# Two load buffers of their own for modulation weights, and a down projection that moves 512 columns

## The chip, the cores and the metric

The kernel runs on one core of a Trainium2 chip, as one program. The metric is device time in microseconds, from the start to the end of an execution. Of the core's engines, TensorE (PE) multiplies, VectorE (DVE) and ScalarE (ACT) work element by element, GpSimd (POOL) does little here, and SyncE (SP) only issues transfers: all of the kernel's transfers stand in its one queue, in program order, and one that waits for a buffer holds those behind it.

## What is computed

Two layers of a backbone over 512 latent tokens and 256 context tokens with 1024 channels. Each layer has shift, scale and gate vectors from a small product with `w_mod` ("modulation"), three token mixers (retention, attention, mLSTM) with a gated merge and an output projection, and a gated MLP:

```
mod_l = split((silu_c @ w_mod[l] + b_mod[l])[:, None, :], 6)
pl = split_proj(modulate(x, mod_l[0], mod_l[1]) @ w_in[l] + b_in[l])
...
x = layer_norm(alpha * x + mod_l[2] * mix_l, ln1_g[l], ln1_b[l])
ffn_l = conv_ffn(modulate(x, mod_l[3], mod_l[4]), w_up[l], conv_w[l], conv_b[l], w_down[l])
x = layer_norm(alpha * x + mod_l[5] * ffn_l, ln2_g[l], ln2_b[l])
```

In `conv_ffn` the hidden layer has 2816 features, and its last product is `(silu(g) * a) @ w_down`. In layer 0 context tokens are carried along (768 tokens); layer 1 needs outputs for the 512 latent tokens alone.

## The kernel before

**Products.** Every large product is made in three passes of a reduced 32-bit format: the operand is split into a high part and a rest (`xh`, `xl`; `ah`, `al`; weights `wh`, `wl`), and high x high, high x rest, rest x high are summed in PSUM. A block of weights, up to 128 x 1024 numbers or 512 KB, comes by `wload` (L302) into a buffer `raw`; `wblock` (L308) makes `wh` from it by a cast on ScalarE (L313) and `wl` by a subtraction on VectorE (L314). There are five `raw` buffers and two each of `wh` and `wl`. All of TensorE's matmuls are issued at L214, in `mm`.

**Modulation.** `mod_unit` (L341) makes 256 columns of one vector. It takes two halves of 512 KB, four matmuls each, 32 x 256, in full fp32, which read `raw` itself (no cast); the trace shows two records for each. A `raw` buffer of a half is free when TensorE has run its four matmuls. Four units gather in one PSUM bank `pp`; `flush_mod` sums them (`pm`) and writes the vectors. Forty-eight units are made: eight at the start, eight one by one in the mixer of layer 0 (`tmod(0, 4)`, L1274 and on), four at once before its merge (L1391), twenty-four in `finish` (L1065), and four at its end in layer 1.

**finish** is the layer norm after each sub-layer, tile by tile (128 tokens). For each tile it ends with `post` (L1069): modulation units (`tmod(*mi[2:])`, two of them in layer 0's first norm and at the seam of the layers, one in layer 1), then eight transposes (`ptr`) of the normalised tile `xn` into the next product's operand. At the seam it also writes the finished tile to memory (`dr_x`, L1475).

**Down projection** (`tm`, L463, called from L1498). The features come in groups of 5, 5, 6 and 6; after the up projection of a group its share of the down projection is added to the residual. The activations are the stationary operand, the weights move, 256 columns at a time: for each quarter of the columns two blocks of weights (n - 2 features, then two), over six token tiles in layer 0, four in layer 1, two tiles to a PSUM bank, three banks `g`. `accumulate` (L1109) takes each bank out with two VectorE operations. The last group goes tile by tile and also makes the statistics of the norm.

**Order.** TensorE's order is written out by `Mixer` (L150): a foreground generator, and background ones (mixers, `finish`, `gate_rows`) that get a step when their due time, in estimated TensorE microseconds, has come. The order on the other engines and in SyncE's queue is made by a scheduler when the program is built, with `wload` at high priority.

Of the kernel before, what the change touches and what calls it, by code (L numbers as in the profile page):

```python
# [9 lines left out]
F32 = mybir.dt.float32  # L10
# [3 lines left out]
OP = mybir.AluOpType  # L14
# [5 lines left out]
DEPTH = 2  # L20
# [73 lines left out]
def layout(inputs):  # L94
    f = {k: np.asarray(v) for k, v in inputs.items()}
    A = {}
    A["x"] = f["x"].reshape(SEQ, D)
    A["ctx"] = f["ctx"].reshape(CTX, D)
    A["cT"] = np.stack([f["c"].reshape(8, 128).T, f["c_ctx"].reshape(8, 128).T], axis=2)
    w = f["w_mod"].reshape(DEPTH, 2, 4, 128, 24, 256)  # L100
    A["wmod"] = w.transpose(0, 4, 1, 3, 2, 5).reshape(DEPTH, 24, 2, 128, 1024)
    A["bmodT"] = f["b_mod"].reshape(DEPTH, 6, 8, 128).transpose(0, 3, 1, 2).reshape(DEPTH, 128, 48)
    w_in, b_in = f["w_in"], f["b_in"]
    glb = np.zeros((DEPTH, 128), np.float32)
    for dst, src in ((0, O_LI), (32, O_LI + 4), (64, O_LF), (96, O_LF + 4)):
        glb[:, dst:dst + 4] = b_in[:, src:src + 4]
    fm = [w_in[:, :, c:c + 128] for c in FM_COLS]
    A["wfm"] = np.stack([b.reshape(DEPTH, 8, 128, 128).transpose(0, 2, 1, 3).reshape(DEPTH, 128, 1024) for b in fm], 1)
    A["bfm"] = np.stack([glb] + [b_in[:, c:c + 128] for c in FM_COLS], 2)
    A["wtm"] = np.stack([w_in[:, :, c:c + 256].reshape(DEPTH, 2, 4, 128, 256).transpose(0, 1, 3, 2, 4)  # L110
                         .reshape(DEPTH, 2, 128, 1024) for c in TM_COLS], 1)
    vg = np.concatenate([w_in[:, :, TM_COLS[1]:TM_COLS[1] + 256], w_in[:, :, O_LI:O_LI + 16]], 2)
    A["wvg"] = vg.reshape(DEPTH, 8, 128, 272).transpose(0, 2, 1, 3).reshape(DEPTH, 128, 2176)
    A["btm"] = np.stack([b_in[:, c:c + 256] for c in TM_COLS], 1)
    w = np.stack([f["w_br_mlstm"], f["w_br_ret"], f["w_br_att"]], 1).reshape(DEPTH, 3, 4, 128, 4, 256)
    A["wbr"] = w.transpose(0, 1, 4, 3, 2, 5).reshape(DEPTH, 3, 4, 128, 1024)
    w = f["w_out"].reshape(DEPTH, 2, 4, 128, 4, 256)
    A["wout"] = w.transpose(0, 4, 1, 3, 2, 5).reshape(DEPTH, 4, 2, 128, 1024)
    w = f["w_up"].reshape(DEPTH, 8, 128, 2 * NF, 128)
    A["wup"] = w.transpose(0, 3, 2, 1, 4).reshape(DEPTH, 2 * NF, 128, 1024)  # L120
    w = f["w_down"].reshape(DEPTH, NF, 128, 4, 256)
    A["wdn"] = w.transpose(0, 3, 2, 1, 4)
    A["convT"] = np.stack([f["conv_w"][:, i].reshape(DEPTH, 2 * NF, 128).transpose(0, 2, 1) for i in range(3)]
                          + [f["conv_b"].reshape(DEPTH, 2 * NF, 128).transpose(0, 2, 1)], 3).reshape(DEPTH, 128, 8 * NF)
    A["gnT"] = np.concatenate([f["mlstm_gn_g"].reshape(DEPTH, 4, 128).transpose(0, 2, 1),
                               f["ret_gn_g"].reshape(DEPTH, 4, 128).transpose(0, 2, 1)], 2)
    A["qkg"] = np.concatenate([f["attn_qn_g"], f["attn_kn_g"]], 1)
    dl = f["ret_decay_logit"]
    t = np.zeros((DEPTH, 128, 16), np.float32)
    for d in range(2):  # L130
        for j in range(2):
            t[:, :64, 2 * d + j] = dl[:, d, 2 * j, None]
            t[:, 64:, 2 * d + j] = dl[:, d, 2 * j + 1, None]
        for h in range(4):
            t[:, :, 4 + 4 * d + h] = dl[:, d, h, None]
            t[:, 64 * d:64 * d + 64, 12 + h] = dl[:, d, h, None]
    A["dlog"] = t
    for n in ("ln1_g", "ln1_b", "ln2_g", "ln2_b"):
        A[n] = f[n]
    A["cst"] = _constants()  # L140
    return {k: np.ascontiguousarray(v) for k, v in A.items()}
# [62 lines left out]
def _program(es, nc, tc, I, OUT):  # L204
# [3 lines left out]
    def mm(out, lhsT, rhs, **kw):  # L208
        n = 1
        for d in out.shape[1:]:  # L210
            n *= d
        r = {F32: 1.7, BF: 0.43}.get(rhs.dtype, 0.425 if n >= 256 else 1.7)
        M.cost(n * r / 1e3)
        nc.tensor.matmul(out, lhsT, rhs, **kw)  # L214
# [28 lines left out]
    def pt(name="p"):  # L243
        return psp.tile([128, 512], F32, name=name, tag="p")

    def gt(name="g"):
        return psg.tile([128, 512], F32, name=name, tag="g")
# [51 lines left out]
    dr_v = [dr.tile([128, 6, 128], F32, name=f"dr_v{i}") for i in range(4)]  # L299
    dr_a = dr.tile([6, 128, 768], F32, name="dr_a")  # L300

    def wload(src, n=1024):  # L302
        raw = wp.tile([128, 1024], F32, name="raw", tag="raw", bufs=5)
        with tc.high_priority():
            M.wdma = SP.dma_start(out=raw[:, :n], in_=src)
        return raw

    def wblock(src, n=1024):  # L308
        raw = wload(src, n)
        h = wp.tile([128, 1024], F32R, name="wh", tag="wh", bufs=2)  # L310
        l = wp.tile([128, 1024], F32R, name="wl", tag="wl", bufs=2)
        with tc.high_priority():
            S.copy(h[:, :n], raw[:, :n])  # L313
            V.tensor_tensor(l[:, :n], raw[:, :n], h[:, :n].bitcast(F32), op=OP.subtract)  # L314
        return h, l
# [25 lines left out]
    def mod_unit(l, idx, q):  # L341
        u = len(mod_tail) % 4
        keep = (l, idx) not in ((0, 2), (0, 3))
        if len(mod_tail) == 4:
            flush_mod()
        if not keep or u == 0:
            held.append(pt("pp"))
        pp = held[0]
        for half in range(2):
            raw = wload(I["wmod"][l, idx * 4 + q, half]).rearrange("p (k n) -> p k n", k=4)  # L350
            for k in range(4):
                mm(pp[32 * k:32 * k + 32, :256], sc_[:, 4 * half + k, 6 - 2 * u:38 - 2 * u], raw[:, k, :],
                   start=(half == 0 and not (keep and u)), stop=(half == 1), skip_group_check=True)
        M.cost(-2.4)
        if keep:
            mod_tail.append(((l, idx, q), None))
            if u == 3:
                mod_tail[0] = (mod_tail[0][0], mod_part())
            return
        if u == 0:  # L360
            part = mod_part()
        else:
            part = mod_tail[0][1]
            V.tensor_tensor(part, held.pop()[:, :256], part, op=OP.add)
        mod_tail.append(((l, idx, q), part))
# [97 lines left out]
    def tm(srcs, lhs, tiles, nks, evac, hook=None, w=256):  # L463
        per = 512 // w
        banks = [tiles[i:i + per] for i in range(0, len(tiles), per)]
        gs = [None] * len(banks)
        tot = sum(nks)
        done = 0
        for src, nk in zip(srcs, nks):
            h, l = src() if callable(src) else wblock(src, nk * w)  # L470
            for bi, ts in enumerate(banks):
                if hook:
                    yield from hook(int(done > 0), ts)
                if done == 0:
                    gs[bi] = gt()
                for i, t in enumerate(ts):
                    for k, pi in [(k, pi) for k in range(nk) for pi in (0, 1)] + [(k, 2) for k in range(nk)]:
                        mm(gs[bi][:, w * i:w * i + w], lhs(done + k, t, pi == 1), (l if pi == 2 else h)[:, w * k:w * k + w],
                           start=(done + k == 0 and pi == 0 and i == 0),
                           stop=(done + k == tot - 1 and pi == 2), skip_group_check=True)  # L480
                    yield
                if done + nk == tot:
                    evac(ts, gs[bi][:, :w * len(ts)].rearrange("p (t c) -> p t c", c=w))
            done += nk

    def x_lhs(xh, xl):
# [622 lines left out]
    def accumulate(l, X, xslot, ts, g, q, rows, first, final):  # L1109
        hf, co = divmod(q, 2)  # L1110
        i = 0
        while i < len(ts):
# [11 lines left out]
                    V.bn_stats(bst[:, u, 6 * q:6 * q + 6], X[:, xslot(u), 256 * q:256 * q + 256])  # L1124
            i += n

    LAT, ALL = ((0, 512),), ((0, 512), (512, 768))

    def layer(l, xT, key):
# [301 lines left out]
        for gr, (go, gnum) in enumerate(zip(GOFF, GROUPS)):  # L1431
# [50 lines left out]
            def keep(q, si, src):  # L1482
# [12 lines left out]
                        kept[q, si] = h, m  # L1495
                return kept[q, si]

            for ts in (((0, 1), (2,), (3,)) if final and last else trips if final else (tuple(range(nqt)),)):  # L1498
                for q in range(4):
                    n0 = gnum - 2  # L1500
                    srcs = [I["wdn"][l, q][:, go:go + n0].rearrange("p k c -> p (k c)"),
                            I["wdn"][l, q][:, go + n0:go + gnum].rearrange("p k c -> p (k c)")]
                    if final and last:
                        srcs = [functools.partial(keep, q, si, src) for si, src in enumerate(srcs)]
                    yield from tm(srcs, alh, ts, (n0, 2), lambda tt, g: accumulate(l, X, xslot, tt, g, q, rows, gr == 0, final))
                if final:
                    M.done.update(f"{key2}.acc{t}" for t in ts)
# [30 lines left out]
```

## Time and profile before

| | us |
|---|---|
| median of 3 runs | 2524.01 (2521.85 to 2524.84) |
| the profiled execution, its own time | 2534.83 |
| its span, first to last instruction | 2533.0 |
| TensorE busy | 2435.9 |
| VectorE busy | 1574.9 |
| ScalarE busy | 1002.7 |

The profile is of one execution. Its rows give the time of an instruction from the span's start; "busy" is the union of an engine's instructions. Matmuls overlap in the records, so the pitch of a stream is read from a count in a stretch, not from the duration of one. The granted clock is a share of TensorE's full 2.4 GHz; 0.5 is the lower level, 1.2 GHz.

### The profile page before, as it was taken

The numbers are of one execution on the slowest core, as the hardware profiler recorded it, in microseconds if no ns is written. First come the engines' busy times: TensorE is split into PE (matmuls) and PEld (weight loads), VectorE is DVE, ScalarE is ACT, GpSimd is POOL, SyncE is SP. The second block draws the span as 40 slices with busy tenths as digits, with TensorE's granted clock in tenths as the row PEclk, the third lists the DMA queues.
The fourth block names the chain that finished last, engine by engine and source line by source line (L and its number), as shares of the span: only waits on it lengthen the run. The fifth ranks groups of instructions, "written<-read, shape, count | busy, mean of one in ns | idle before, by whom it ended". The sixth has DMA issues, their size and how long they took to land.

```text
span 2533.0 us, 41667 instructions
## 1 busy us (share of the span) xinstructions
PE 2435.9 (96%) x16552; PEld 2155.9 (85%) x16552; DVE 1574.9 (62%) x3308; ACT 1002.7 (40%) x1802; POOL 92.2 (4%) x111
## 2 busy tenths in 40 slices
PE   6999999999899999999999989999999989999998
PEld 4977998888788988999998878779787788988887
DVE  5556465545477885555545773767565877855557
ACT  4433321455433473232313353434254455633332
POOL 1000001000000000000000010000110000000000
PEclk9999999999999999999999999999999998999999
DMA  7253524322554562212121383354434444533232
GB/s 257 90 171 134 167 94 140 111 82 86 175 165 165 193 243 84 74 53 77 53 76 55 125 292 126 99 172 140 161 122 146 135 134 167 176 105 99 83 106 67
DMA packets 147651, 329.21 MB, mean 130 GB/s; under 512 B 15872, under 2 KB 59136, under 8 KB 147456
## 3 DMA queue, kind: packets, MB, share of 16 engines
q1 hardware_dynamic: 147456, 326.54, 39.4%
q8 instruction: 131, 2.15, 0.4%
q14 instruction: 64, 0.52, 0.1%
HBM read 283.49 MB, written 42.99 MB: 129 GB/s over the span
## 4 chain that ended last, share of the span: by engine, by line
PE 85%; DVE 7%; DMA 4%; ACT 3%; issue 1%; POOL 0%; SPq 0%; DVEq 0%; ACTq 0%; POOLq 0%
PE g L214 72%; PE pAV L214 2%; PE psc L214 2%; PE pPT L218 2%; DVE wl L314 2%; DMA raw<-in_wmod_dram 1%; PE pE L214 1%; PE pNf L214 1%; ACT wh L313 1%; PE pp L214 1%; PE pU L214 1%; DMA raw<-in_wtm_dram 1%; PE pO L214 1%; DMA raw<-in_wup_dram 1%; PE pyt L218 0%
## 5 line engine op out<-in xcount | busy, mean ns | idle before, releaser
L214 PE MATMUL g<-xh,wh 128*128 128x512 f32 (+1 forms) x2448 | 827.9, 353 | 11.0 <-ACT xh L1315 4.7
L214 PE MATMUL g<-xl,wh 128*128 128x512 f32 (+1 forms) x2448 | 814.8, 348 | 1.4 <-DVE xl L442 0.8
L314 DVE TENSOR_TENSOR wl<-raw,wh 128x1024 fp32r<-128x1024 f32 (+3 forms) x358 | 411.9, 1151 | 354.5 <-ACT wh L313 270.8
L313 ACT CAST wh<-raw 128x1024 fp32r<-128x1024 f32 (+3 forms) x358 | 355.2, 992 | 644.4 <-PE g L214 575.5
L214 PEld LDWEIGHTS g<-xh,wh 128*128 128x128 f32 x2448 | 466.7, 191 | 80.2 <-issue 10.0
L214 PEld LDWEIGHTS g<-xl,wh 128*128 128x128 f32 x2448 | 468.0, 191 | 57.3 <-DVE xl L1316 1.3
L214 PE MATMUL g<-xh,wl 128*128 128x512 f32 (+1 forms) x2448 | 511.1, 348 | 3.0 <-DVE wl L314 3.0
L214 PEld LDWEIGHTS g<-xh,wl 128*128 128x128 f32 x2448 | 402.4, 191 | 61.1 <-DVE wl L314 3.4
L214 PE MATMUL g<-wh,ah 128*128 128x256 f32 x808 | 207.3, 284 | 3.6 <-ACT ah L1459 3.6
L214 PE MATMUL g<-wh,al 128*128 128x256 f32 x808 | 206.5, 283 | 2.7 <-DVE al L1460 2.7
L214 PE MATMUL g<-wh,xh 128*128 128x256 f32 (+1 forms) x768 | 203.4, 295 | 3.1 <-ACT wh L313 1.7
L214 PE MATMUL g<-wh,xl 128*128 128x256 f32 (+1 forms) x768 | 199.1, 290 | 3.4 <-DVE xl L1377 2.1
L214 PEld LDWEIGHTS g<-wh,ah 128*128 128x128 f32 x808 | 153.9, 190 | 4.9 <-ACT ah L1459 4.2
L214 PEld LDWEIGHTS g<-wh,xh 128*128 128x128 f32 x768 | 150.9, 196 | 8.2 <-issue 3.3
L214 PEld LDWEIGHTS g<-wh,al 128*128 128x128 f32 x808 | 153.9, 190 | 4.1 <-DVE al L1460 3.5
L214 PEld LDWEIGHTS g<-wh,xl 128*128 128x128 f32 x768 | 151.1, 197 | 4.2 <-DVE xl L1377 2.4
L1420 ACT ACTIVATE tc<-g,conv 128x512 f32<-128x512 f32 (+1 forms) x142 | 96.8, 682 | 132.8 <-PE g L214 131.6
L214 PE MATMUL g<-wl,ah 128*128 128x256 f32 x808 | 144.9, 283 | 0.8 <-DVE wl L314 0.8
L1421 DVE SCALAR_TENSOR_TENSOR tc<-g,conv,tc 128x511 f32<-128x511 f32 (+1 forms) x142 | 88.7, 625 | 83.8 <-ACT tc L1420 83.1
L414 POOL TENSOR_TENSOR rstd<-veps,mhalf 128x1 f32<-128x1 f32 (+3 forms) x68 | 71.8, 1057 | 1797.6 <-DVE veps L412 1783.2
L947 ACT ACTIVATE Pe<-psc,mx 128x256 f32<-128x256 f32 (+1 forms) x144 | 80.7, 565 | 142.2 <-DVE mx L942 96.7
L214 PE MATMUL g<-wl,xh 128*128 128x256 f32 (+1 forms) x768 | 129.1, 289 | 0.9 <-DVE wl L314 0.8
(279 smaller groups left out, 3159.0 us busy)
## 6 DMA issues: line engine op xcount, KB each, us to landing
raw<-in_wup_dram SPq DMA_DIRECT2D x108, 512.0 KB, 3.5
raw<-in_wmod_dram SPq DMA_DIRECT2D x96, 512.0 KB, 5.4
raw<-in_wfm_dram SPq DMA_DIRECT2D x80, 512.0 KB, 3.6
raw<-in_wtm_dram SPq DMA_DIRECT2D x32, 512.0 KB, 5.3
raw<-in_wout_dram SPq DMA_DIRECT2D x32, 512.0 KB, 3.6
raw<-in_wbr_dram SPq DMA_DIRECT2D x28, 512.0 KB, 4.3
dr_g<-stg SPq DMA_DIRECT2D x48, 256.0 KB, 2.0
raw<-in_wdn_dram SPq DMA_DIRECT2D x20, 512.0 KB, 3.6
```

The source lines that it names most:

```text
L214: nc.tensor.matmul(out, lhsT, rhs, **kw)
L218: nc.tensor.transpose(out, in_, ident)
L313: S.copy(h[:, :n], raw[:, :n])
L314: V.tensor_tensor(l[:, :n], raw[:, :n], h[:, :n].bitcast(F32), op=OP.subtract)
L414: G.tensor_tensor(r, t, mhalf[:, :n], op=OP.pow)
L947: S.activation(pe[:, a:b], prs[si][:, :b - a], AF.Exp, bias=mx[:, 3:4], scale=0.125, accum_out=sm[:, si:si + 1])
L1420: S.activation(t[:, a:b], g, AF.Identity, bias=conv[:, jj, 3:4], scale=conv[:, jj, 1:2])
L1421: V.scalar_tensor_tensor(t[:, a + 1:b], g[:, :b - a - 1], conv[:, jj, 0:1], t[:, a + 1:b], op0=OP.mult, op1=OP.add)
```

## The change

`wload` gets a tag: products keep three buffers `raw`; modulation halves get two of their own, `mraw`, except at the start, where the first two vectors (shift and scale of layer 0) use both kinds in turn. The first three feature groups of the down projection (`if not final`) go through a new function `tm_wide`: weights in a layout `wdw` with halves of 512 columns, blocks of two features (2, 2, 1 or 2, 2, 2), one PSUM bank per token tile, from the pools `g` and `p` (`gx`) in turn, and an eviction of 512 columns per tile.

```diff
-    def wload(src, n=1024):
-        raw = wp.tile([128, 1024], F32, name="raw", tag="raw", bufs=5)
+    def wload(src, n=1024, tag="raw"):
+        raw = wp.tile([128, 1024], F32, name=tag, tag=tag, bufs=3 if tag == "raw" else 2)
...
         for half in range(2):
-            raw = wload(I["wmod"][l, idx * 4 + q, half]).rearrange("p (k n) -> p k n", k=4)
+            tag = "raw" if (l, idx) < (0, 2) and (q + idx + half) % 2 == 0 else "mraw"
+            raw = wload(I["wmod"][l, idx * 4 + q, half], tag=tag).rearrange("p (k n) -> p k n", k=4)
...
+    def tm_wide(srcs, lhs, tiles, nks, evac):
+        gs = {}
+        tot = sum(nks)
+        done = 0
+        for src, nk in zip(srcs, nks):
+            h, l = wblock(src, nk * 512)
+            for i, t in enumerate(tiles):
+                if done == 0:
+                    gs[t] = gt() if i % 2 == 0 else pt("gx")
+                for k, pi in [(k, pi) for k in range(nk) for pi in (0, 1)] + [(k, 2) for k in range(nk)]:
+                    mm(gs[t], lhs(done + k, t, pi == 1), (l if pi == 2 else h)[:, 512 * k:512 * k + 512],
+                       start=(done + k == 0 and pi == 0), stop=(done + k == tot - 1 and pi == 2))
+                yield
+                if done + nk == tot:
+                    evac(t, gs.pop(t))
+            done += nk
...
+    def accumulate_wide(X, xslot, t, g, hf, rows, first):
+        tmp = stg()[:, :512]
+        V.tensor_tensor(tmp, g, rows[int(t >= 4)][hf], op=OP.mult)
+        xs = X[:, xslot(t), 512 * hf:512 * hf + 512]
+        V.scalar_tensor_tensor(xs, xs, ALPHA if first else 1.0, tmp, op0=OP.mult, op1=OP.add)
...
+            if not final:
+                for hf in range(2):
+                    srcs = [I["wdw"][l, hf][:, k:min(k + 2, go + gnum)].rearrange("p k c -> p (k c)")
+                            for k in range(go, go + gnum, 2)]
+                    yield from tm_wide(srcs, alh, range(nqt), [s.shape[1] // 512 for s in srcs],
+                                       lambda t, g: accumulate_wide(X, xslot, t, g, hf, rows, gr == 0))
+                continue
```

On TensorE nothing but the down projection of these groups changes: 1920 matmuls of 256 columns go, 960 of 512 come. The two-unit steps of `post` stand as 16 matmuls `pp` in a row before and after, the four units before the merge as 32. SyncE's queue does change. First, its loads around the layer norm inside layer 0 (`wout` output projection, `wup` up projection, `wmod` modulation). Before:

```order
L305 DMA raw<-in_wout_dram 128x1024 x3
L305 DMA raw<-in_wmod_dram 128x1024 x4
L305 DMA raw<-in_wout_dram 128x1024 x2
L305 DMA raw<-in_wmod_dram 128x1024 x4
L305 DMA raw<-in_wout_dram 128x1024 x3
L305 DMA raw<-in_wmod_dram 128x1024 x4
```

and with the change:

```order
L307 DMA raw<-in_wout_dram 128x1024 x8
L307 DMA mraw<-in_wmod_dram 128x1024 x2
L307 DMA raw<-in_wout_dram 128x1024
L307 DMA mraw<-in_wmod_dram 128x1024 x2
L307 DMA raw<-in_wout_dram 128x1024
L307 DMA mraw<-in_wmod_dram 128x1024 x2
L307 DMA raw<-in_wup_dram 128x1024
L307 DMA mraw<-in_wmod_dram 128x1024 x2
```

The four halves of a step stood together; now they come by twos, each two behind the run of the two before, with product loads between.

Second, the same queue at the seam of the layers, around the steps of the second and third tile (`dr_x` the finished tile's write, `wdn` down projection, `wtm` the next layer's input projection). Before:

```order
L305 DMA raw<-in_wmod_dram 128x1024 x4
L1475 DMA dr_x<-xres 128x1024
L305 DMA raw<-in_wdn_dram 128x512
L305 DMA raw<-in_wdn_dram 128x1024
L305 DMA raw<-in_wdn_dram 128x512
L305 DMA raw<-in_wmod_dram 128x1024 x3
L1475 DMA dr_x<-xres 128x1024
L305 DMA raw<-in_wmod_dram 128x1024
L305 DMA raw<-in_wtm_dram 128x1024 x3
```

and with the change:

```order
L307 DMA mraw<-in_wmod_dram 128x1024 x3
L1501 DMA dr_x<-xres 128x1024
L307 DMA mraw<-in_wmod_dram 128x1024
L307 DMA raw<-in_wdn_dram 128x512
L307 DMA raw<-in_wtm_dram 128x1024
L1501 DMA dr_x<-xres 128x1024
L307 DMA mraw<-in_wmod_dram 128x1024 x2
L307 DMA raw<-in_wtm_dram 128x1024
L307 DMA mraw<-in_wmod_dram 128x1024 x2
L307 DMA raw<-in_wtm_dram 128x1024 x2
L307 DMA mraw<-in_wmod_dram 128x1024 x2
```

The second pair of the second tile's step now stands behind a `dr_x` write and a product load; before, one of its four loads stood behind a write of that kind.

## Rows read from the trace of the kernel before

**Rows 1.** The page: span, and each engine's busy time.

```profile
span 2533.0 us, 41667 instructions
...
PE 2435.9 (96%) x16552; PEld 2155.9 (85%) x16552; DVE 1574.9 (62%) x3308; ACT 1002.7 (40%) x1802; POOL 92.2 (4%) x111
```

**Rows 2.** TensorE's waits, whole span: us in total, times, longest us.

```profile
PE pp L214 <- DMA raw<-in_wmod_dram: 20.9, 14, 3.3
PE ptr L218 <- ACT xn L1102: 10.5, 5, 4.5
```

**Rows 3.** Stretches: start:end, length, busy (count) by engine, granted clock, DMA, GB/s.

```profile
1117.00:1157.00 40.00, 40.00 (x343) 40.00 (x342) 21.40 (x31) 7.11 (x9) 0.00 (x0) 1.00 0.26 83
...
2292.00:2322.00 30.00, 28.46 (x226) 28.05 (x225) 16.32 (x24) 6.70 (x10) 0.00 (x0) 0.94 0.35 111
...
2240.00:2285.00 45.00, 45.00 (x201) 37.27 (x200) 25.66 (x31) 19.69 (x25) 0.00 (x0) 1.00 0.28 85
```

**Rows 4.** TensorE's waits from 2200 to 2325, down projections of layer 1.

```profile
PE g L214 <- DVE al L1460: 1.3, 2, 0.7
PE g L214 <- ACT ah L1459: 0.9, 1, 0.9
```

**Rows 5.** Timeline, TensorE: start, us, what; a two-unit step in layer 0.

```profile
853.80 1.93 PE L214 MATMUL pp<-raw,silc 128*32 128x256 f32 x32
```

**Rows 6.** Timeline: one unit in the mixer of layer 0, and loads behind it.

```profile
142.05 1.07 PE L214 MATMUL pp<-raw,silc 128*32 128x256 f32 x16
142.75 0.82 SPq L305 DMA_DIRECT2D raw<-in_wmod_dram  x2
```

**Rows 7.** Modulation loads, issue to landing: stretches 130 to 202, 845 to 930, 1440 to 1522.

```profile
DMA to landing us min/median/max: 3.3/4.4/5.8
...
DMA to landing us min/median/max: 3.2/6.0/8.2
...
DMA to landing us min/median/max: 3.9/6.8/9.5
```

**Rows 8.** Timeline at the seam: a step, a tile's write, the load behind it.

```profile
1461.44 1.93 PE L214 MATMUL pp<-raw,silc 128*32 128x256 f32 x32
...
1466.78 0.33 SPq L1475 DMA_DIRECT2D dr_x<-xres  x1
1469.91 0.33 SPq L305 DMA_DIRECT2D raw<-in_wmod_dram  x1
```

**Rows 9.** Timeline, TensorE: the four units before the merge, and matmuls after.

```profile
669.26 2.37 PE L214 MATMUL pp<-raw,silc 128*32 128x256 f32 x40
...
678.75 1.08 PE L214 MATMUL pp<-raw,silc 128*32 128x256 f32 x8 [0.18 <-DMA raw<-in_wmod_dram]
...
682.29 0.63 PE L214 MATMUL g<-xh,wh 128*128 128x512 f32 x1
682.71 0.63 PE L214 MATMUL g<-xl,wh 128*128 128x512 f32 x1
```

**Rows 10.** TensorE's waits from 1448 to 1527, the seam of the layers.

```profile
PE ptr L218 <- ACT xn L1102: 5.8, 3, 3.1
PE pp L214 <- DMA raw<-in_wmod_dram: 3.3, 1, 3.3
PE g L214 <- ACT wh L313: 1.7, 1, 1.7
PE g L214 <- DVE wl L314: 1.6, 2, 0.8
```

**Rows 11.** Timeline, TensorE: the last step at the seam, its fourth half.

```profile
1520.55 1.08 PE L214 MATMUL pp<-raw,silc 128*32 128x256 f32 x8 [3.28 <-DMA raw<-in_wmod_dram]
```

**Rows 12.** Stretches behind three waits, with the granted clock.

```profile
676.00:688.00 12.00, 8.90 (x37) 6.17 (x38) 5.64 (x8) 4.96 (x10) 0.00 (x0) 0.57 1.04 397
901.00:906.00 5.00, 4.27 (x22) 4.04 (x23) 5.00 (x12) 4.84 (x10) 0.00 (x0) 0.66 0.84 342
1491.00:1501.00 10.00, 7.25 (x39) 7.26 (x40) 6.52 (x14) 6.98 (x12) 0.36 (x1) 0.66 0.89 337
```

More of the change, by code (lines that the diff above doesn't have):

```diff
@@ L122, in layout @@
     A["wdn"] = w.transpose(0, 3, 2, 1, 4)
+    w = f["w_down"].reshape(DEPTH, NF, 128, 2, 512)
+    A["wdw"] = w.transpose(0, 3, 2, 1, 4)
     A["convT"] = np.stack([f["conv_w"][:, i].reshape(DEPTH, 2 * NF, 128).transpose(0, 2, 1) for i in range(3)]
```

## The prediction

> **What bounds the kernel now.** I read the page first: TensorE is busy 96% of the span [rows 1]. So the time is TensorE's own instructions, its waits, and the stretches in which its clock is low. Next, the list of TensorE's waits [rows 2]: the longest entry is the small modulation matmuls (pp), which wait 20.9 us for their own weight loads; the transposes (ptr) wait 10.5 us for xn. Then the stretches. In the down projection (256 columns) and in the up projection of layer 1 (512 columns) TensorE has no gap, so 40.00 us over 343 matmuls and 45.00 over 201 give the pitch: 0.117 us for 256 columns, 0.224 for 512 [rows 3].
>
> **Part one: 512 columns in the down projection.** Three of four feature groups hold 16 of 22 features. Before: 16 features x 10 token tiles (6 and 4) x 4 column blocks x 3 products = 1920 matmuls of 256 columns; after, 960 of 512. A pair of the old ones takes 2 x 0.117 = 0.233 us, a new one 0.224: 960 x 0.009 = **-9 us**, all on the path, since nothing else bounds these stretches. The new blocks hold two features each, where the old ones began with three or four. In layer 1 TensorE waits 2.2 us for the last features' ah and al at the starts of these stages [rows 4], and one such wait is followed by a granted clock of 0.94 over 30 us [rows 3], 1.8 us of lost clock. The third block, which needs the fifth feature, now starts two blocks (some 11 us) later, so I count another -3. Sum **-12**, bounds -9 and -16. The evictions keep their number and size (12 a group in layer 0, each two VectorE operations on 512 columns) but come six in a row where three did; VectorE is busy about half of these stretches [rows 3], and six banks instead of three stand between an eviction and the bank's next use, so I price that at nothing. If that cover fails, a bank waits for its eviction and the 12 us shrink. The casts (12 fewer on ScalarE, 12 on VectorE) lie beside TensorE.
>
> The Trainium skill has a rule that speaks against this part: "TensorE: Matmul & The Clock Gate", section "Wait — 56ns, not 53.3ns?", puts a warm matmul at its columns over 2.4 GHz plus about 2.5 ns. By that a pair of 256 would take 218 ns and one of 512 216 ns, and this part would be worth 2.4 us instead of 9. The rows differ from the page by more at 256 columns than at 512, and I go by the rows.
>
> **Part two: two buffers for modulation.** A unit has two halves of 512 KB, which the fp32 matmuls read straight from the load buffer; the buffer is free when TensorE has run that half. Five shared buffers become three for products and two for modulation. TensorE's order of units does not change, and there lies the matter: twelve times it runs two units (four halves) back to back, at the end of each layer norm tile (six in layer 0, six at the seam of the layers), and once four units (eight halves). Before, the four halves were loaded ahead: a group took 1.93 us without a gap [rows 5]. With two buffers, halves three and four cannot even be issued until one and two have run, and nothing on TensorE stands between.
>
> What such a reload costs is seen in the mixer of layer 0, where pairs are issued just after a unit has run: the unit starts at 142.05, the two loads go out from 142.75 for 0.82 us [rows 6], so the second at about 1.1 us after the start, and twelve such loads took 3.3, 4.4 and 5.8 us to land (least, median, most) [rows 7]. In the two busier stages the median is 6.0 and 6.8 [rows 7], but there four or five were under way together. I take 5.1 for the second of a pair: 1.1 + 5.1 + 0.5 for its matmuls = 6.7 us a group instead of 1.93, +4.8; twelve groups: **+58**. Lower bound: 3.3 us, +3.0 a group, 36. Upper: 6.4, +6.1, 73.
>
> SyncE's queue adds to it. At the seam the second pair stands behind two more product loads and behind writes of the finished layer norm tile (second excerpt of the order). Before, the same mixture shows what that costs: a group began at 1461.44, the tile's write went out at 1466.78, and the modulation load behind it only at 1469.91 [rows 8]. Two of the twelve groups have such a write in front of their second pair that is not due before they start. I take **+8** (0 to 16).
>
> The eight halves: before, five were there and three were reloaded; it took from 669.26 to the end of the last piece at 678.75 + 1.08, or 10.6 us [rows 9]. Now six are reloaded in three rounds of 6.2 us, plus 1.1 for the last pair: 19.7, **+9** (4 to 14).
>
> What goes in return are waits at these same places, since ScalarE and VectorE catch up while TensorE stands: at the seam ptr for xn 5.8, the modulation load 3.3, wh 1.7 and wl 1.6 [rows 10], and in layer 0 the rest of ptr's 10.5 [rows 2], 4.7: 17.1 in all. I take **-15** (-8 to -17).
>
> The clock: waits of 3 to 5 us are followed here by stretches at the lower of the two levels, 1.2 GHz. The means 0.57, 0.66 and 0.66 over 12, 5 and 10 us [rows 12] are 10, 3.4 and 6.8 us of it, and matmuls of 512 columns then start every 0.43 us (682.29 to 682.71) [rows 9]. So 3.4 us cost up to 1.6. Each new wait is as long as these; at 1.5 us a group that is 18, less about 10 for the 20 us that these stretches have already: **+8** (-8 to +30).
>
> The first 57 us use both kinds of buffer alternately, five loads at once as before: 0 (3 either way). The products' three buffers stand behind two converted blocks, and the shortest block lasts 24 x 0.117 = 2.8 us, so a load goes out several blocks ahead, against landings of 3.3 to 5.8: nothing, and if that cover went it would show as waits for wh. The single units (mixer of layer 0, end of layer 1) have a block of products between them: nothing.
>
> **Sum:** -12 + 58 + 8 + 9 - 15 + 8 = **+56 us**. It is made against the profiled execution, 2534.8 us (span 2533.0 [rows 1]), 10.8 above the median of 2524.0; put on the median, **2580 us**.
>
> **Rivals.**
> - *Worse at the queue and in the clock.* Four groups, not two, wait some 5 us for a write in front of their second pair, and every group is followed by the longer low-clock stretch: +12 and +25 more, or 2617. For it: dr_x and dr_v writes stand between the pairs all through the seam. Against it: most of them are due before the group.
> - *Mild.* Reloads land at the shortest time (36 for the twelve) in a quiet queue, all 17 us of waits are covered, no clock is lost, the eight halves cost 4 and the queue 8: -12 + 36 + 4 + 8 - 17 = +19, 2543. Against it: only the quickest of the reloads took 3.3 us.
> - *Faster.* Product loads no longer queue behind modulation halves, and the second pairs land under waits that TensorE has anyway: -12, and -7 for the waits on modulation loads, wh and wl at the seam, 2505. The point that decides: a group may expose at most (12 + 15) / 12 = 2.2 us. Against it: even a 3.3 us landing exposes 3.0; and the one group that has a late fourth half already shows it bare: 3.28 us of idle in front of it [rows 11].
> - *No difference.* Gain and loss happen to cancel, or the order leaves the second pair less late than I read it: 2524.
>
> The rule that speaks for the faster rival is the Trainium skill's, "Trainium Kernel Development and Optimization", section "Best Practices": "Double-buffer for performance", overlap the loads with compute. Two buffers of their own are just that; by that rule the loads would be hidden and the faster rival's time come out. No row shows a reload hidden inside a group.
>
> **How the numbers follow.** Forecast (2560 to 2605): 0.63; worse: 0.18; mild: 0.10; faster: 0.06; no difference: 0.03. A measurement of this kernel tells about 0.2% (5 us) from no change. Slower is the first three, 0.91. The range is 2545 to 2622: forecast, most of mild, half of worse.
>
> **What would show it.** In the profile after: pp waits for its load some 70 us in all instead of 20.9, in two pieces within each four-half group, which then lasts 6 to 8 us; ptr hardly waits for xn; a granted clock below 1 behind most groups; 960 matmuls of 512 columns at 0.224 us with no wait for ah or al in the first three groups of layer 1. I am wrong if the groups last under 4 us, if wh or wl waits grow elsewhere (three product buffers too few), or if the down projection waits for banks.

## The result, and the profile after

The changed kernel takes 2600.17 us (median of 4 runs, 2596.17 to 2601.56); the kernel before takes 2524.43 beside it (2521.85 to 2532.82). The ratio is 1.0284, interval 1.0263 to 1.0305: slower. The forecast was 2580 us, with a range of 2545 to 2622. Between the two profiled executions, on which the sum was made, the difference is 2599.80 - 2534.83 = 65.0 us, where the sum said 56.

The page of the changed kernel, as [rows 1]:

```profile
span 2598.0 us, 39687 instructions
...
PE 2451.1 (94%) x15592; PEld 2116.3 (81%) x15592; DVE 1571.9 (61%) x3296; ACT 1001.6 (39%) x1790; POOL 91.8 (4%) x111
```

TensorE has 960 matmuls fewer and is busy 15.2 us longer; with 65.0 us more span it is idle 50 us longer. Its waits over the whole span, to be held against [rows 2]:

```profile
PE pp L216 <- DMA mraw<-in_wmod_dram: 79.0, 30, 7.6
...
PE g L216 <- DVE wl L316: 4.9, 2, 3.0
...
PE pp L216 <- DMA raw<-in_wmod_dram: 3.2, 2, 3.0
...
PE g L216 <- ACT wh L315: 1.2, 1, 1.2
...
PE ptr L220 <- ACT xn L1122: 0.7, 1, 0.7
```

The modulation matmuls (pp) wait 82.2 us for their loads, 61.3 more than before; the transposes (ptr) wait 9.8 less for xn. The casts (wh, wl) are waited for no more than before, so three product buffers starve nothing. One step of two units, TensorE first, then SyncE's queue, against [rows 5] and [rows 6]:

```profile
860.73 1.07 PE L216 MATMUL pp<-mraw,silc 128*32 128x256 f32 x16
865.26 1.08 PE L216 MATMUL pp<-mraw,silc 128*32 128x256 f32 x8 [3.46 <-DMA mraw<-in_wmod_dram]
866.52 1.08 PE L216 MATMUL pp<-mraw,silc 128*32 128x256 f32 x8 [0.18 <-DMA mraw<-in_wmod_dram]
```

```profile
861.43 0.80 SPq L307 DMA_DIRECT2D mraw<-in_wmod_dram  x2
```

The first unit runs at once; 0.70 us after its start the two reloads go out, and the second unit comes in two pieces when they have landed. The step takes 6.88 us where one took 1.93. The landings of all modulation loads in two stretches (845 to 970, layer 0's norm, and then 1484 to 1600, the seam), 24 each, of which the reloads are half, against [rows 7]:

```profile
DMA to landing us min/median/max: 3.6/4.5/6.2
```

```profile
DMA to landing us min/median/max: 3.5/4.9/7.6
```

At the seam, one of the longest steps, against [rows 8] and [rows 11]: SyncE's queue, then TensorE.

```profile
1547.51 0.49 SPq L1043 DMA_DIRECT2D brow<-in_btm_dram  x1
1548.12 0.84 SPq L307 DMA_DIRECT2D mraw<-in_wmod_dram  x2
1549.01 0.78 SPq L307 DMA_DIRECT2D raw<-in_wtm_dram  x1
1549.85 0.65 SPq L1501 DMA_DIRECT2D dr_x<-xres  x1
1550.60 0.73 SPq L307 DMA_DIRECT2D raw<-in_wtm_dram  x1
```

```profile
1547.42 1.07 PE L216 MATMUL pp<-mraw,silc 128*32 128x256 f32 x16
1554.70 1.08 PE L216 MATMUL pp<-mraw,silc 128*32 128x256 f32 x8 [6.21 <-DMA mraw<-in_wmod_dram]
```

The reloads go out 0.70 us after the start here too. They aren't held in the queue: they take 6.5 and 7.4 us to land, with two product loads and the tile's write issued right behind them. The four units before the merge, against [rows 9]:

```profile
667.09 1.07 PE L216 MATMUL pp<-mraw,silc 128*32 128x256 f32 x16
674.07 2.31 PE L216 MATMUL pp<-mraw,silc 128*32 128x256 f32 x16 [5.91 <-DMA mraw<-in_wmod_dram]
680.83 2.31 PE L216 MATMUL pp<-mraw,silc 128*32 128x256 f32 x16 [4.45 <-DMA mraw<-in_wmod_dram]
686.54 1.08 PE L216 MATMUL pp<-mraw,silc 128*32 128x256 f32 x8 [3.40 <-DMA mraw<-in_wmod_dram]
687.78 1.08 PE L216 MATMUL pp<-mraw,silc 128*32 128x256 f32 x8 [0.16 <-DMA mraw<-in_wmod_dram]
```

Three rounds of reloads, as counted: 21.8 us to the end of the last piece, against 10.6. And the waits at the seam, 1484 to 1600, against [rows 10]: pp has taken over what ptr had.

```profile
PE pp L216 <- DMA mraw<-in_wmod_dram: 31.7, 11, 6.4
PE g L216 <- DVE wl L316: 2.0, 1, 2.0
PE g L216 <- ACT wh L315: 1.2, 1, 1.2
```

Where the 65 us lie is read best from the lengths between five marks on TensorE that the kernels here share: the first two-unit step, the first down projection, the first step at the seam, layer 1's first down projection, the end (starts from the timelines, us). The experiments told of below stand beside it.

| | to the first step | norm in layer 0 | to the seam | seam, and mixers of layer 1 | rest of layer 1 | span |
|---|---|---|---|---|---|---|
| before | 853.8 | 135.9 | 459.3 | 757.9 | 326.1 | 2533.0 |
| after | 860.7 | 167.9 | 456.6 | 793.0 | 319.7 | 2598.0 |
| bufs_only | 864.1 | 170.1 | 458.0 | 793.4 | 324.1 | 2609.8 |
| wide_shared | 850.4 | 135.3 | 455.6 | 755.4 | 319.5 | 2516.1 |
| no_reload | 865.0 | 135.6 | 456.6 | 746.5 | 321.2 | 2525.0 |
| two_three | 868.0 | 152.5 | 456.6 | 776.9 | 325.0 | 2579.1 |
| filler | 860.3 | 162.5 | 455.1 | 787.6 | 319.6 | 2585.0 |

The loss is in the two layer norms (+32.0, +35.1) and in the stretch with the piece before the merge (+6.9); the two stretches with down projections gain 2.7 and 6.4.

### The profile page after: what moved, and what is told of

The parts are those of the page before. It is cut to its first block, busy times and chain, and to the rows that moved or that the text cites. A ratio compares the mean times of both kernels' runs of the same rounds, so it can differ in the third digit from the quotient of the medians.

```text
span 2598.0 us, 39687 instructions
## 1 busy us (share of the span) xinstructions
PE 2451.1 (94%) x15592; PEld 2116.3 (81%) x15592; DVE 1571.9 (61%) x3296; ACT 1001.6 (39%) x1790; POOL 91.8 (4%) x111
## 5 line engine op out<-in xcount | busy, mean ns | idle before, releaser
L216 PEld LDWEIGHTS g<-xh,wh 128*128 128x128 f32 x2448 | 466.5, 191 | 78.3 <-issue 10.8
L216 PE MATMUL pp<-mraw,silc 128*32 128x256 f32 x704 | 64.8, 473 | 84.5 <-DMA mraw<-in_wmod_dram 79.0
L216 PE MATMUL g<-wh,ah 128*128 128x256 f32 (+1 forms) x328 | 109.4, 347 | 3.9 <-ACT ah L1485 2.7
L216 PEld LDWEIGHTS pp<-mraw,silc 128*32 128x32 f32 x704 | 18.0, 120 | 114.4 <-DMA mraw<-in_wmod_dram 101.8
L216 PE MATMUL g<-wh,al 128*128 128x256 f32 (+1 forms) x328 | 108.0, 343 | 1.4 <-DVE al L1486 1.4
L216 PEld LDWEIGHTS g<-wl,xh 128*128 128x128 f32 x768 | 108.5, 194 | 0.1
```

## Experiments

The theory: the time is lost where TensorE runs units back to back that the two buffers cannot hold, and the 512 columns gain a little. Rivals: the wide down projection itself costs (banks, clock); three product buffers are too few; the loads stand too late in SyncE's queue.

**Each part alone.** First the wide down projection with five shared buffers (wide_shared):

```diff
-        raw = wp.tile([128, 1024], F32, name=tag, tag=tag, bufs=3 if tag == "raw" else 2)
+        raw = wp.tile([128, 1024], F32, name=tag, tag=tag, bufs=5)
...
-            tag = "raw" if (l, idx) < (0, 2) and (q + idx + half) % 2 == 0 else "mraw"
+            tag = "raw"
```

> The 512-column down projection stays, the five load buffers are shared again. Theory (the reload inside back-to-back units costs the time, the down projection gains a little): 2512 to 2522 us, under the kernel before by 2 to 12; the matmuls of 512 columns start every 0.232 us as in the changed kernel, so the pitch gives about 3 of it and the rest comes from layer 1's waits for ah and al. Rival (the wide down projection itself lowers the clock or waits for banks): over 2535 us.

Measured: 2515.74 us (2514.26 to 2518.30; before 2527.53), ratio 0.9961, interval 0.9948 to 0.9973: 0.4% faster, little but clear of the interval. This version beats both kernels. Then the buffers alone (bufs_only), with the block `if not final: ... tm_wide ... continue` taken out:

> The split of the buffers, three and two, stays; the down projection is the old one, 256 columns. Theory: all of the loss and none of the gain, 2603 to 2615 us. Rival (the wide down projection is part of the loss, by its clock or because its blocks need more loads ahead): under 2590 us.

Measured: 2608.8 us (2606.48 to 2611.57), ratio 1.0328 (1.0314 to 1.0342). So the loss is the buffers' alone, and the wide down projection gives some 9 us of it back with split buffers and 12 with shared ones.

**Is it the reload?** In no_reload, of each two-unit step the second unit reads the first one's buffers:

```diff
-            raw = wload(I["wmod"][l, idx * 4 + q, half], tag=tag).rearrange("p (k n) -> p k n", k=4)
+            if not again[0]:
+                raws[half] = wload(I["wmod"][l, idx * 4 + q, half], tag=tag).rearrange("p (k n) -> p k n", k=4)
+            raw = raws[half]
...
+                again[0] = n == 2 and i == 1
                 mod_unit(*modq.pop(0))
```

> In the twelve steps of two units the second unit reads the halves of the first again: 24 loads of 512 KB and the second unit's own weights are left out, the matmuls stay. Theory (the loss of the twelve steps is the reload alone): each step takes 2 to 3 us, and of the 65 us that the two layer norms lost all comes back, 2525 to 2545 us; the eight halves before the merge still take about 20 us. Rival (three buffers are too few for products, or the lower clock has another cause): over 2565 us.

Measured: 2523.06 us (2520.58 to 2526.78). Every step is whole again:

```profile
865.04 1.93 PE L216 MATMUL pp<-mraw,silc 128*32 128x256 f32 x32
```

The norm in layer 0 takes 135.6 us (table), as with five shared buffers, though products still have three buffers. So three are enough for them, and the steps' loss is the reload. The total came out 2 us below the expected range: the stretch of the seam takes 746.5 us, with 24 loads fewer in all, where wide_shared takes 755.4.

**Is it the lack of work between the units?** In split_units the second unit of a step is issued later; nothing is left out.

```diff
-            tmod(*mi[2:])
+            tmod(*mi[2:4])
...
+            late = prev and mi[4] == 2
...
             prev = (t, xn)
-            yield 7.0
+            if late:
+                yield 3.5
+                tmod(*mi[2:4])
+                yield 3.5
+            else:
+                yield 7.0
         if prev:
             post(*prev)
+            if mi[4] == 2:
+                yield 3.5
+                tmod(*mi[2:4])
```

> The buffers stay three and two, and nothing is left out: the second unit of each step is issued some 28 product matmuls after the first, instead of right behind it. Theory (a reload needs about 5 us, and only the lack of TensorE work between the units shows it): most of it is hidden, pieces of 0 to 2 us are left, 2530 to 2560 us. Rival (the loads stand too late in the queue, whatever stands between the units, or there are too few product buffers): over 2575 us.

Measured: 2541.11 us (2538.09 to 2550.6), ratio 1.0066. Two units of this kernel, 36 matmuls apart, on TensorE:

```profile
870.39 1.07 PE L216 MATMUL pp<-mraw,silc 128*32 128x256 f32 x16
...
875.84 0.64 PE L216 MATMUL pp<-mraw,silc 128*32 128x256 f32 x8
877.56 0.64 PE L216 MATMUL pp<-mraw,silc 128*32 128x256 f32 x8 [1.08 <-DMA mraw<-in_wmod_dram]
```

With 4.4 us of products in between, 1.08 us is left of a wait that was over 3. Against wide_shared, which has five shared buffers, the changed kernel is 84 us slower; 59 of these are back, with the same five buffers and the same loads. The lateness in the queue is not the cause: in the changed kernel the reloads of all twelve steps go out 0.7 to 0.8 us after the start. Of the 24 us by which the span is still longer than wide_shared's, 10.0 lie before the first step, 9.6 in the norm of layer 0 and 3.6 at the seam, where two units still meet once (9.56 us); in that norm 2.7 us of waits for loads are left, and where the rest of its 9.6 comes from is not shown.

**How many buffers a step needs.** two_three gives the modulation three of the five and the products two, one_four four and one (only the number in `bufs=` differs).

> Of the five buffers the products keep two and the modulation halves get three. Theory: the third half of a group is then there ahead, and the fourth goes out alone when the first has run, 0.7 us into the group, lands some 4.2 us later and is run in 0.5: groups of about 5.4 us instead of 7.7, so 2560 to 2580 us, with two buffers enough for the products. Rival (the buffer that the products lose is missed): over 2590 us, with more than 20 us of waits for wh and wl on TensorE.

Measured: 2584.42 us (2580.86 to 2590.2), ratio 1.0222. A step there, on TensorE:

```profile
868.03 1.50 PE L216 MATMUL pp<-mraw,silc 128*32 128x256 f32 x24
872.49 0.64 PE L216 MATMUL pp<-mraw,silc 128*32 128x256 f32 x8 [2.96 <-DMA mraw<-in_wmod_dram]
```

Three halves run, the fourth is waited for: 5.10 us, 5.4 expected. The twelve steps take 69.2 us in all, against 93.0 with two buffers. The total is 4 us above the expected range, which left out two things. The two product buffers also serve the first vectors, and the first step comes 7.3 us later (table). And the rest of layer 1 takes 5.3 us more: in its last down projection TensorE waits 1.72 us for a block of weights whose cast is named xh there (L1518), and the granted clock of that stretch is 0.92, against 1.00 in the changed kernel. Waits for wh and wl stay small, 6.9 us in all.

> One buffer for the products, four for the modulation halves. Theory (a step's four halves must be there before it begins): the twelve steps take 2 us again, as with five shared buffers. Against that each product block's load can only go out when the block before is converted, and then takes 4 to 6 us: hidden behind the longer blocks (5 to 8 us), not behind the blocks of 3 us. I expect the steps back at 2 us, waits for wh and wl of 20 to 80 us in all, and 2540 to 2600 us. If two buffers for the products were already too few, over 2600 us.

Measured: 2787.75 us (2787.1 to 2799.84), far outside. Half of the theory holds: the steps are whole, but for the first (3.62 us) and the fifth (2.22). The other half, that one product buffer would make 20 to 80 us of waits, doesn't. TensorE's waits, and one step:

```profile
PE g L216 <- ACT wh L315: 150.5, 79, 6.4
```

```profile
915.59 1.93 PE L216 MATMUL pp<-mraw,silc 128*32 128x256 f32 x32
```

With one buffer, a block's load can only go out when the block before it is cast. The clock is lower too: its mean over the run is 0.955, in the changed kernel 0.972, and TensorE is busy 2531.6 us on as many instructions, there 2451.1. From two product buffers to one is the step that costs; from three to two costs some 5 us in the last down projection, beside the start.

**Is the piece before the merge worth mending?** Its reloads cost time before the change too [rows 9]. shared_spread is wide_shared with its four units issued one by one inside the merge:

```diff
-        tmod(0, 4, 4)
         yield from merge(0, qseg)
...
                     yield from fm(blk, yh, yl, segs, ev, nk=4, kb=4 * (bi % 2), co=128 * i, w=256)
+                    if bi == 0 and i == 1:
+                        tmod(0, 4)
```

> Five shared buffers and the 512-column down projection as in wide_shared; the four units that ran back to back before the merge of layer 0 are issued one by one inside it. Theory (back-to-back units beyond the five buffers cost a reload before the change as well): the 10.1 us of that piece become four times 1.1, and a stretch at the lower clock goes, 2505 to 2511 us against 2515.7. Rival (TensorE would wait at the merge anyway): 2513 to 2518 us, with new waits for the merge's weights or operands.

Measured: 2527.88 us (2520.39 to 2530.82): 12 above wide_shared, outside the theory's range and the rival's. TensorE's waits from 640 to 705, of wide_shared and then of shared_spread:

```profile
PE pp L216 <- DMA raw<-in_wmod_dram: 4.5, 3, 3.0
PE g L216 <- ACT wh L315: 1.4, 1, 1.4
PE pPT L220 <- ACT Pe L967: 0.3, 1, 0.3
```

```profile
PE pPT L220 <- ACT PT L984: 5.1, 1, 5.1
PE g L216 <- ACT xh L1341: 3.5, 3, 2.3
PE pPT L220 <- DVE Qo L944: 1.4, 1, 1.4
PE g L216 <- DVE xl L1342: 1.2, 3, 0.5
```

The four units stood where TensorE would otherwise wait for the merge's operands (xh, xl) and the attention's PT: 4.5 us of waiting for a load went, and the other waits grew from 1.7 to 11.2. The first step comes 6.5 us later, which is most of the 10.4 by which the spans differ. split_all does the same on top of split_units:

> Three and two buffers, with the twelve steps split as in split_units and the four units before the merge issued one by one inside it. Theory (two buffers of their own cost only where two units meet): the 24 us piece before the merge goes, 2514 to 2526 us; what is left above the shared buffers is the last step at the seam, where two units still meet. Rival (three product buffers cost something of their own): over 2530 us.

Measured: 2541.32 us (2535.06 to 2545.41), the same as split_units and outside the range, though its piece of 24 us is gone: from there to the first step 16.5 us of waits for loads went, 9.4 of waits for PT, xh and other operands came, and the first step comes at 860.6 us, in split_units at 860.4. And shared_two leaves two of the four units in place:

> As wide_shared, with two of the four units before the merge left in place and two issued inside it. The four halves fit the five buffers. Theory after shared_spread (the units before the merge stand where TensorE would wait for the merge's operands and the attention's PT anyway): between the two, 2515 to 2524 us. If the reloads of the last three halves were the cost and a 2 us piece covers enough, under 2513 us.

Measured: 2527.69 us (2522.45 to 2532.81), above both expected ranges. Its first down projection comes 8.1 us later than in wide_shared; that its median lies 12 us above, while the profiled spans differ by 4.6, stays open.

**What the lower clock costs.** filler puts work that nobody reads where TensorE waits:

```diff
+            if n == 2 and i == 1 and modq and modq[0][:2] <= (l, idx):
+                for _ in range(12):
+                    nc.tensor.matmul(held[0][:, 256:384], ones, ident, start=False, stop=False, skip_group_check=True)
```

> The changed kernel, with 12 matmuls of 128 x 128 in full fp32 between the two units of each of the twelve steps; they write columns of the bank that nobody reads, some 2.6 us of work, less than the 3.3 us that TensorE at least waits there. Theory (the waits also cost by the lower clock behind them, the part of the loss that I priced at 8): the steps take as long as before, 6.4 to 9.9 us, most of the stretches at the lower clock behind them go, 2580 to 2592 us against 2600. Rival (the lower clock falls on waits, or does not come from the idle time): 2597 to 2605 us.

Measured: 2590.98 us (2586.8 to 2597.08), ratio to before 1.0258. A step, on TensorE:

```profile
903.82 1.07 PE L216 MATMUL pp<-mraw,silc 128*32 128x256 f32 x16
904.82 2.94 PE L376 MATMUL pp<-ident,ones 128*128 128x128 f32 x24
908.11 0.64 PE L216 MATMUL pp<-mraw,silc 128*32 128x256 f32 x8 [0.35 <-DMA mraw<-in_wmod_dram]
```

The stretches of the two norms in the kernel before, in the changed kernel and then with the filler (the granted clock is the number behind the last bracket):

```profile
845.00:1030.00 185.00, 179.94 (x1354) 161.46 (x1353) 133.37 (x262) 92.46 (x155) 9.63 (x12) 0.99 0.48 165
1425.00:1620.00 195.00, 178.99 (x1353) 161.39 (x1352) 130.55 (x314) 88.07 (x146) 13.95 (x22) 0.96 0.55 185
```

```profile
845.00:1030.00 185.00, 160.49 (x1079) 135.74 (x1078) 119.39 (x240) 88.70 (x148) 9.64 (x12) 0.92 0.47 154
1425.00:1620.00 195.00, 157.74 (x1192) 140.17 (x1191) 105.30 (x228) 67.62 (x115) 12.66 (x21) 0.87 0.48 156
```

```profile
845.00:1030.00 185.00, 172.45 (x1245) 148.84 (x1244) 122.08 (x243) 89.49 (x150) 9.67 (x12) 0.99 0.48 161
1425.00:1620.00 195.00, 170.79 (x1396) 156.87 (x1395) 107.39 (x240) 68.60 (x116) 12.77 (x21) 0.96 0.52 166
```

The twelve steps take no less (95.9 us in all, 93.0 without the filler), and the clock of the two stretches is back at 0.99 and 0.96. The median is 9 us lower, with useless work added. That alone is not clear of the noise, since the two ratios' intervals overlap (1.0263 to 1.0305 without, 1.0224 to 1.0291 with it); but of the 13.0 us by which the profiled spans differ, 5.4 and 5.4 lie in the two stretches with the norms (table), and the clock tells where. Behind two of the changed kernel's steps:

```profile
867.00:873.00 6.00, 6.00 (x41) 5.47 (x34) 1.53 (x6) 3.46 (x10) 0.28 (x1) 0.67 0.60 182
1557.00:1563.00 6.00, 6.00 (x41) 6.00 (x38) 2.92 (x10) 5.19 (x12) 0.55 (x1) 0.71 0.66 251
```

Over the 6 us behind each of its twelve steps the granted clock is 0.65 to 0.83, 18.5 us of clock lost in all; with the filler it is 1.00 behind six steps and 0.72 to 0.83 behind the others, 8.6 us lost; before the change it was 3.7. So the lower clock behind the waits costs the changed kernel some 9 to 11 us that the filler brings back, 12 or more with the 2.9 that the steps grew; an estimate from the lost clock, 18.5 less 3.7, is 15.

**Why a matmul of 512 columns takes 0.232 us here.** bank_runs is wide_shared with the banks taken in runs:

```diff
-                    gs[t] = gt() if i % 2 == 0 else pt("gx")
+                    gs[t] = gt() if i < 3 else pt("gx")
```

> As wide_shared, but the token tiles of the wide down projection take their banks in runs (three of one pool, then three of the other) instead of in turn. If the turn between the pools is what makes a matmul of 512 columns start every 0.232 us here and every 0.227 us in the up projection, the pitch falls to 0.227 or 0.228; if it is the operands or where they lie, it stays at 0.231 to 0.235.

Measured, in a single run: 2520.28 us, and the pitch didn't fall: the down projection of the second group takes 42.03 us, in wide_shared 42.02. The turn of the banks is not the cause; what is, stays open.

## Why the prediction was right, and where it was off

Direction, mechanism and most signs came as forecast: pp waits of 82 us (some 70 were said), two pieces in each step, no ptr wait to speak of, the clock below 1 behind the steps, no wait for ah or al in the first three down projections of layer 1. The sign that failed is the pitch of the 960 matmuls, 0.232 us instead of 0.224. Term by term, against the profiled execution:

| term | said | measured | from |
|---|---|---|---|
| 512 columns | -12 | -8.7 | lengths of the six down projections |
| twelve steps, with the queue | +58 +8 | +65.9 | 93.0 against 27.1 us in all |
| eight halves | +9 | +11.2 | 21.8 against 10.6 |
| start | 0 | -2.2 | start of the eight halves; 664.8 to 669.6 in five kernels that share this part |
| returned waits | -15 | -12.6 | ptr 10.5 to 0.7, wh 4.0 to 1.2 |
| clock | +8 | about +12 | filler (15 by the lost clock) |
| sum | +56 | +65.6 | measured 65.0 |

The prediction put the wait that the last step at the seam had before (3.28 us [rows 11]) under the returned waits; in the table it stands with the steps. Moved over, the steps are +69.8 and the returned waits -16.5. wl, which the prediction also counted there, did not go (4.6 us before, 4.9 after).

- **The step's price was right.** In layer 0 a step takes 6.96 us on average, 6.7 said; no_reload and split_units show that it is the reload and the missing work between. Its parts made up for each other: the second reload landed after 4.8 us on average, 5.1 said, and from the landing to the end of the step went 1.1 us, 0.5 said. The rule of the faster rival, the Trainium skill's "Double-buffer for performance" ("Trainium Kernel Development and Optimization", "Best Practices"), did not bring that rival's time: the loads are hidden here when there is work to overlap (split_units, for the most part) and when the buffers hold the whole step (wide_shared); two buffers for four halves in a row hide little, 3.2 to 6.5 us of wait stay bare in each step.
- **The queue term: right size, wrong mechanism.** I had two groups wait behind a write in SyncE's queue. The reloads go out on time, in all twelve steps. At the seam they land later: the second reload of a step after 4.6 to 7.6 us, 6.2 on average, with four to nine other transfers under way; in layer 0 after 4.8 on average, with three or four. So all six steps of the seam are longer, 8.55 us on average, and not two. That the neighbours make the landing longer is read from this coincidence; no run tested it. That the term's size fitted is luck.
- **The pitch was mis-sized: about -4, not -9.** The down projection of the second group, in the kernel before and then in the changed one (first and last start of each kind):

```profile
L214 PE MATMUL g<-wh,ah x120: 274/282/286, 1116.2 to 1158.0; 128*128 128x256 f32 x120
L214 PE MATMUL g<-wl,ah x120: 277/279/286, 1116.9 to 1158.4; 128*128 128x256 f32 x120
```

```profile
L216 PE MATMUL g<-wh,ah x30: 389/396/404, 1154.1 to 1194.6; 128*128 128x512 f32 x30
...
L216 PE MATMUL gx<-wl,ah x30: 390/396/398, 1156.4 to 1195.8; 128*128 128x512 f32 x30
```

  By starts, 359 intervals in 42.2 us are 0.1175 each, a pair 0.235; 179 in 41.7 are 0.233. By this group the difference is 0.002 x 960 = 2 us, and it is the group that shows least: over all six, without the few starts that come late by more than a quarter, a pair took 0.2362 on average and the new matmul takes 0.2321, which makes 0.0041 x 960 = 4 us. What made 9 of it is that I took the 512-column pitch from the up projection, where other operands move; by starts it is 0.2265 there. A second fault hardly counts: I divided a stretch by the matmuls counted in it, of which those across its edges count too [rows 3], and that made both pitches too small, by 0.002 for a pair and 0.003 for one of 512. The Trainium skill's figures ("TensorE: Matmul & The Clock Gate", "Wait — 56ns, not 53.3ns?") gave 2.4 us for this part. The 4 us measured lie nearer to that than to 9; its 216 ns for one matmul don't agree (232 measured).
- **The waits for ah and al were worth 3 to 5.** Layer 1's three down projections went from 29.9, 32.1 and 34.3 us to 28.4, 27.9 and 33.7: -6.2, of which the pitch is 1.5 (384 matmuls). The second one alone, with the wait and the clock of 0.94 behind it [rows 3], gives 4.1. But in bufs_only, which keeps the old projection and its waits, that one took 30.6 us: 1.5 of the gain is a stretch of lower clock that differs between executions.
- **The step onto the median was off by more than any term.** The profiled execution before lay 10.8 us above its median, the one after lies on it. I carried +56 over to the median unchanged, which assumes that the changed kernel's profiled execution would lie as far above its own. Of the 20 us between forecast and result, 11 are from there and 9 from the sum.

## What to carry to other kernels

Buffers of their own for one kind of load help only if they hold what the consumer takes in one go, or if the consumer has other work between; count the burst, not the average. A shared pool lends all its buffers to the burst, and that was worth 81 us (bufs_only against the kernel before) to 84 us (the changed kernel against wide_shared) here, with the same memory. Before a wait is mended, look at which wait would stand there without it: the loads' waits before the merge could go entirely and nothing was won.

## What the runs showed of the hardware

In the second group's wide down projection of the changed kernel the starts of consecutive matmuls are 225 to 242 ns apart, within a block of two features in a pattern that comes again every 12 matmuls (two tiles) to within a few nanoseconds; in the up projection of layer 1 (2310 to 2355) every matmul of 512 columns starts 226 or 227 ns after the last. Another order of the banks didn't bring the first to the second. And useless matmuls in the waits brought the granted clock of the two norms from 0.92 and 0.87 to 0.99 and 0.96, with a median 9 us lower.
